# Queries, keys and values by seven block products instead of eight

## The chip, the cores and the metric

The kernel runs on one core of a Trainium2 chip. The metric is the device time of one execution in microseconds. Three runs of the kernel before took 2755.23, 2757.62 and 2761.46 us, with the median at 2757.62.

## What is computed

A backbone of two layers over 1024 latent tokens of width 1024 on a grid of 16 x 64, with 256 context tokens as a prefix. Layer 0 mixes by a gated linear recurrence and a Fourier block, layer 1 by attention in a neighbourhood plus all context keys. Each layer ends with a SwiGLU FFN of hidden size 2816. Everything is float32. The change concerns the start of layer 1's mixer:

```python
def _na_mixer(hx, hc, w_qkv, rpb, w_out, need_ctx):
    qkv = (hx @ w_qkv).reshape(B, R, GRID_W, 3, NA_HEADS, NA_HD)
    q = qkv[:, :, :, 0] * scale
    k = qkv[:, :, :, 1]
    v = qkv[:, :, :, 2]
    qkv_c = (hc @ w_qkv).reshape(B, L, 3, NA_HEADS, NA_HD)
    ...   # scores of 8 x 16 neighbours and 256 context keys, softmax, values, output projection
```

hx is the modulated RMSNorm of the tokens (1024 x 1024), hc that of the context, and w_qkv is 1024 x 3072. Of the context only keys and values are used.

## The kernel before

All products are float32 made of two parts each: an operand is split into a rounded part hi and the rest lo, and mm3 (lines 342 to 346) issues three products, hi with hi, hi with lo and lo with hi, into one bank of PSUM. split (line 308) makes hi on ScalarE (line 310) and lo on VectorE (line 311). A split operand of 512 columns is a tile of 4 KB a partition. 28 of these, called u, make the pool units; wide token rows and loaded blocks take the same tiles. Weights arrive in four staging tiles r of 2 KB, loaded by SP's queue and split into u ahead of their use; class Ahead keeps the loads four and the splits two items ahead. In PSUM the pool ps_main has four banks each for the tags d and g.

The kernel is written as a program of tiles. A planner orders the instructions of each engine by readiness and by program order and sets the waits; memory of a closed pool is used again as soon as the tiles that lay there are done. Pools stack from a left and a right side of SBUF.

The stages in order are: layer 0's mixer, its output projection, gate and up (ffn_up), down (ffn_down), queries, keys and values (qkv), attention, its output projection, and layer 1's FFN. ffn_up and layer 1's down stage (ffn_down1) already use seven block products for eight: Blocks makes the token operands B11, B21, B22 and the combinations T1 to T4 (first for tokens 0 to 511, second for 512 to 1023), Weights makes the sums S1 to S4 from the gate and up columns on GpSimd and splits them, and the loop of ffn_up forms seven products of four contraction tiles each and adds them up on VectorE and GpSimd.

ffn_down(0) multiplies in tok_block: a first block of tokens 0 to 511 with the context, then tokens 512 to 1023. Between its products it runs fillers, one every few steps: in the first block the modulation vectors of layer 1 (mods), in the second turn_steps, which load the finished rows of tokens 0 to 511 and of the context, normalise them (norm_scale), turn them by TensorE (line 1074) and split them after the modulation.

qkv then goes over two token blocks. For each block, 16 tiles of 128 columns of queries and keys are taken in turn, with 8 contraction tiles each (lines 1343 to 1359), the context's 256 columns behind the keys; then the values by tok_block, for which the tokens are the stationary operand. In the first block's values, turn_steps for tokens 512 to 1023 runs as filler. Every weight is loaded and split twice, once for each block. Outputs are split and stored in DRAM as qd, kd and vd. oT, attention's output of 32 KB, is allocated at qkv's start on the left.

attention (line 1375) opens its own pools on the left (qd, kd, bias, s, ot, vd, pt, in this order of memory) and loads for each head queries and keys (prep, line 1406), on SP's queue, by the planner as early as their buffers are free. Its TensorE order is fixed by hand (pin): scores of two tiles, transposes of the weights after softmax, products with the values.

Of the kernel before, what the change touches and what calls it, by code (L numbers as in the profile page):

```python
# [16 lines left out]
P = 128  # L17
D = 1024
T = 1024
# [77 lines left out]
class Blocks:  # L97
# [3 lines left out]
    def __init__(self, kern, l):  # L101
        self.kern, self.l, self.u = kern, l, {}
# [12 lines left out]
    def vectors(self, k):  # L115
        return self.kern.G[self.l][1][:, 0, k:k + 1], self.kern.mt[self.l][:, 3, 0, k:k + 1]
# [6 lines left out]
    def first(self, rows):  # L123

        kern = self.kern
        nc = kern.nc
        xs = [rows[m] for m in range(4)]
        self.kept = []
        for k in range(4):
            r = kern.row()  # L130
            c11, b21 = r[:, :512], r[:, 512:]
            self.kept.append((c11, b21))
            ps = self.turned(xs, k)
            scale, bias = self.vectors(k)
            u = self.unit("B11", k)
            nc.scalar.activation(c11, ps, AF.Copy, scale=scale)
            self.modulated(ps, k, u[:, 0])
            nc.vector.scalar_tensor_tensor(u[:, 1], c11, bias, u[:, 0].bitcast(F32), op0=ALU.add, op1=ALU.subtract)
            self.modulated(self.turned(xs, k + 4), k + 4, b21)
            u = self.unit("B21", k)  # L140
            kern.split(b21, u[:, 0], u[:, 1], "dve")

    def second(self, rows):
# [5 lines left out]
        for k in range(4):  # L149
            r = kern.row()  # L150
# [18 lines left out]
class Weights:  # L169
# [38 lines left out]
    def up(self):  # L208
# [3 lines left out]
        self.u.update({f"S{i}": (u, 0) for i, u in self.s.items()})  # L212

# [50 lines left out]
class Kernel:  # L264
# [797 lines left out]
    def turn_steps(self, ms, src, l, i, units):  # L1062

        nc = self.nc
        n = len(ms) * P
        st = {}

        def load():
            st["x"] = self.load_scale(ms, src)

        def turn(k):
            ps = self.t(self.pp, [P, 512], F32, "g")
            for q, m in enumerate(ms):
                nc.tensor.transpose(ps[:, q * P:(q + 1) * P], st["x"][m][:, k * P:(k + 1) * P], self.ident)
            b = k * n % 512
            if b == 0:
                st["u"] = self.unit()
            u = st["u"][:, :, b:b + n]
            self.modulate_split(ps, l, i, k, ((0, n, int(ms[0] < 0)),), None, u[:, 0], u[:, 1])
            units.setdefault(k, []).append(u)  # L1080

        return [load] + [lambda k=k: turn(k) for k in range(KD)]
# [108 lines left out]
    def ffn_down(self, l, blocks, hd, src, store, gg, fillers=((), ()), start=(0, 0), every=(1, 1)):  # L1191
# [13 lines left out]
        for b, ms in enumerate(blocks):  # L1205
            def act(k, half, b=b, ms=ms):
# [125 lines left out]
    def qkv(self, first, src):  # L1332
        nc, a = self.nc, self.a
        pp = self.pp
        self.kst = ExitStack()
        op_ = self.pool("oT", side="left", stack=self.kst)
        self.oT = [self.t(op_, [P, T], F32, f"oT{j}") for j in range(8)]
        self.vd = self.t(self.dram, [P, 10, 2, 4, 256], F32, "vd")
        self.qd = [self.t(self.dram, [P, 2, T], F32, f"qd{j}") for j in range(8)]
        self.kd = [self.t(self.dram, [P, 2, TT], F32, f"kd{j}") for j in range(8)]  # L1340
        units = first
        for bi, ms in enumerate((BLOCKS[0] + CTX, BLOCKS[1])):
            for mt in range(16):
                w = [self.ws.take() for _ in range(2)]
                for part in range(2 if bi == 0 and mt >= 8 else 1):
# [223 lines left out]
    def run(self):  # L1569
# [64 lines left out]
        def store2(m, x):  # L1634
            nc.sync.dma_start(out=self.x2[m], in_=x)
# [191 lines left out]
```

## Time and profile before

| | us |
|---|---|
| median of three runs | 2757.62 |
| the profiled execution | 2757.91 |
| its span | 2756.1 |
| TensorE busy in it | 2630.0 |
| VectorE busy | 1625.6 |
| ScalarE busy | 1222.3 |
| GpSimd busy | 881.9 |

PE is TensorE's products, PEld its loads of the stationary operand, which run beside them; DVE is VectorE, ACT ScalarE, POOL GpSimd, SP the engine that issues the DMAs. Times in the rows are microseconds from the span's start, unless ns is written. A product's busy time includes its way through the array, so that two in a row overlap; the distance of their starts is what one costs. Behind a row in brackets stands the idle time of the engine before it, and what ended it.

### The profile page before, as it was taken

The page shows a single profiled execution, that of the slowest core. Times are in us where ns is not written, and L with a number is a line of the kernel's source. Part 1 is how long each engine was busy: PE and PEld are TensorE (multiplying, and loading weights), DVE is VectorE, ACT ScalarE, POOL GpSimd, SP SyncE. Part 2 cuts the span into 40 slices and gives each one's busy share as a digit, 9 for nine tenths or more (in the row PEclk, how much of TensorE's full clock was granted, in tenths as well). Part 3 has the DMA queues.
Part 4 walks back from the last instruction along what each step waited for, and adds up shares of the span by engine and source line. Part 5 has one row for each costly group of instructions (what it writes and reads, how often), then busy time and mean ns, then how long its engine had stood idle before and what let it go on. Part 6 is the DMA issues. An engine that isn't in the chain of part 4 may idle for free. (4 is left out here: it accounts for less than half of the span.)

```text
span 2756.1 us, 36241 instructions
## 1 busy us (share of the span) xinstructions
PE 2630.0 (95%) x12914; PEld 2146.4 (78%) x12914; DVE 1625.6 (59%) x2506; ACT 1222.3 (44%) x2201; POOL 881.9 (32%) x794
## 2 busy tenths in 40 slices
PE   7999999899999999899999999999997999999997
PEld 3677577688888887777878887998875888888786
DVE  3765285866543445675552433877767666556966
ACT  3676264422232223343532333988754333333443
POOL 1000014544444341002010000777536554542911
PEclk9999999899999999999999999999999999999999
DMA  7333472233221227855344485777441333235524
GB/s 245 107 113 124 134 250 86 73 104 112 78 75 67 73 67 233 268 163 211 108 172 169 162 254 187 189 179 172 141 138 54 108 107 115 88 108 185 200 100 145
DMA packets 185574, 390.41 MB, mean 142 GB/s; under 512 B 19761, under 2 KB 50097, under 8 KB 183346
## 3 DMA queue, kind: packets, MB, share of 16 engines
q1 hardware_dynamic: 185394, 388.10, 43.5%
q8 instruction: 102, 1.67, 0.2%
q14 instruction: 78, 0.64, 0.1%
HBM read 302.57 MB, written 85.46 MB: 141 GB/s over the span
## 5 line engine op out<-in xcount | busy, mean ns | idle before, releaser
L345 PE MATMUL d<-u,u 128*128 128x512 f32 (+1 forms) x864 | 335.0, 388 | 5.4 <-DVE u L311 5.4
L344 PE MATMUL d<-u,u 128*128 128x512 f32 (+1 forms) x864 | 335.0, 390 | 4.5 <-DVE y L248 2.6
L346 PE MATMUL d<-u,u 128*128 128x512 f32 (+1 forms) x864 | 333.2, 386 | 0.0
L311 DVE TENSOR_TENSOR u<-r,u 128x512 fp32r<-128x512 f32 x309 | 231.5, 765 | 78.2 <-ACT u L310 76.6
L310 ACT ACTIVATE u<-r 128x512 fp32r<-128x512 f32 x309 | 187.7, 626 | 176.0 <-PE d L346 42.9
L346 PE MATMUL g<-u,u 128*128 128x512 f32 x604 | 236.2, 391 | 4.3 <-DVE u L311 4.3
L345 PE MATMUL g<-u,u 128*128 128x512 f32 x604 | 236.5, 391 | 1.8 <-DVE u L311 1.8
L344 PE MATMUL g<-u,u 128*128 128x512 f32 x604 | 236.6, 392 | 0.0
L244 POOL TENSOR_TENSOR ss<-ss 128x1 f32<-128x1 f32 x36 | 13.3, 371 | 654.7 <-ACT junk L242 654.5
L311 DVE TENSOR_TENSOR s<-r,s 128x512 fp32r<-128x512 f32 x176 | 139.0, 794 | 127.3 <-ACT s L310 126.7
L345 PE MATMUL g<-u,s 128*128 128x512 f32 x528 | 208.2, 394 | 4.9 <-POOL u L166 4.8
L344 PE MATMUL g<-u,s 128*128 128x512 f32 x528 | 207.5, 394 | 2.1 <-ACT u L121 1.9
L346 PE MATMUL g<-u,s 128*128 128x512 f32 x528 | 207.0, 392 | 0.0
L344 PEld LDWEIGHTS d<-u,u 128*128 128x128 f32 x864 | 164.4, 190 | 48.1 <-ACT u L310 9.5
L310 ACT ACTIVATE s<-r 128x512 fp32r<-128x512 f32 x176 | 108.6, 629 | 209.1 <-PE g L346 144.5
L345 PEld LDWEIGHTS d<-u,u 128*128 128x128 f32 x864 | 164.5, 190 | 39.9 <-DVE u L311 9.4
L346 PEld LDWEIGHTS d<-u,u 128*128 128x128 f32 x864 | 164.5, 190 | 31.7
L1476 POOL TENSOR_TENSOR s<-s,sm 128x640 f32<-128x640 f32 (+1 forms) x128 | 151.0, 1200 | 61.9 <-DVE sm L1472 56.2
L192 POOL TENSOR_TENSOR r<-rg,ru 128x512 f32<-128x512 f32 x44 | 59.5, 1352 | 305.3 <-DMA rg<-in_w_gu_dram 123.1
L344 PE MATMUL d<-u,ga 128*128 128x512 f32 x352 | 139.3, 396 | 0.1
L346 PE MATMUL d<-u,ga 128*128 128x512 f32 x352 | 138.2, 393 | 0.6 <-DVE ga L311 0.6
L1152 POOL TENSOR_TENSOR ub<-ub,ua 128x512 f32<-128x512 f32 x44 | 72.9, 1657 | 204.6 <-DVE ua L1151 199.0
(407 smaller groups left out, 6511.3 us busy)
## 6 DMA issues: line engine op xcount, KB each, us to landing
mraw<-in_w_mod_dram SPq DMA_DIRECT2D x192, 256.0 KB, 3.6
rg<-in_w_gu_dram SPq DMA_DIRECT2D x44, 512.0 KB, 3.6
ru<-in_w_gu_dram SPq DMA_DIRECT2D x44, 512.0 KB, 3.7
r<-in_w_down_dram SPq DMA_DIRECT2D x88, 256.0 KB, 3.4
x<-x SPq DMA_DIRECT2D x40, 512.0 KB, 4.3
r<-in_w_qk_dram SPq DMA_DIRECT2D x64, 256.0 KB, 3.8
qd<-qd SPq DMA_DIRECT2D x32, 512.0 KB, 11.1
r<-in_w_out_dram SPq DMA_DIRECT2D x48, 256.0 KB, 3.2
```

Source lines behind the costliest of these rows:

```text
L192: pool(rs[3], rg[:, h1], ru[:, h1], op=ALU.subtract)
L244: nc.gpsimd.tensor_tensor(st, ss[:, 0:1], ss[:, 1:2], op=ALU.add)
L310: i = nc.scalar.activation(hi, src, AF.Copy) if eng == "act" else nc.vector.tensor_copy(hi, src)
L311: j = nc.vector.tensor_tensor(lo, src, hi.bitcast(F32), op=ALU.subtract)
L344: nc.tensor.matmul(ps, lhs[0], rhs[0], start=start, stop=False)
L345: nc.tensor.matmul(ps, lhs[0], rhs[1], start=False, stop=False)
L346: nc.tensor.matmul(ps, lhs[1], rhs[0], start=False, stop=stop)
L1152: pool(ub, ub, ua, op=add)
L1476: pin(nc.gpsimd.tensor_tensor(s, s, sm.to_broadcast([P, nl + L]), op=ALU.mult))
```

## The change

The tokens are cut into two halves of 512, the contraction into two halves of 512, and the columns into two: for a pair of 128 query and 128 key columns by query and key (class Pairs, eight pairs j), for the values by column halves of 512. The eight products of blocks become seven of sums of blocks, with the same combinations as in ffn_up. Values come first now (values_of), then queries and keys (queries_and_keys). Each weight is loaded once, or twice where it enters a sum of the values.

Blocks.first is cut into four steps (first_of), which run as fillers in the second block of ffn_down for tokens 0 to 511; turn_steps keeps the context. The rows of tokens 512 to 1023 are normalised where ffn_down stores them (store2) and stay in SBUF; Blocks.second turns and combines them between the two contraction halves of the values. The first product of the values, B11 and B21 with the first 512 columns, runs in d banks together with the context's values in g; the context's second half follows alone; then T1, T2, B22, T3 and T4, each with four weights. The sums of the values' weights are made on GpSimd from the staging tiles (value_loads).

The pools are set in another order: y before mraw, so that mraw can be closed between the two blocks of ffn_down (between) for a pool vu of the values' split weights on the right; a pool v for the values on the left in place of y; after it, on the same memory, the pool uq for the weights of queries and keys (rg, ru, ga, s4, s1, s3, s2, up, 40 KB) and qt above it (p1, ha, hb, ua, ub, and two output tiles qo). oT is allocated in attention. The diff, cut to its core:

```diff
+class Pairs(Weights):
+    def load(self, j):
+        self.raw = [kern.t(kern.uw, [P, 1024], F32, n) for n in ("rg", "ru")]
+        for i in range(2):
+            kern.nc.sync.dma_start(out=self.raw[i], in_=kern.a["w_qk"][8 * i + j])
...
+    def value_loads(self, unit, s1):
+        def sum1(k):
+            a, b = raw(0, 1, k), raw(1, 1, k)
+            pool(s1(k), a, b, op=add)
+            return later(s1(k))
...
+        plain = [lambda r=r, c=c, k=k: self.wload(src(r, c, k), unit) for c in range(2) for r in range(2) for k in range(4)]
+        sums = [lambda f=f, k=k: f(k) for f in (sum1, sum2, sum4, sum3) for k in range(4)]
+        return plain + sums + [lambda k=k: self.wload(src(1, 1, k), unit) for k in range(4)]
...
+    def values_of(self, vp, tb, rows, cx):
+        p1, p5 = ([self.t(vp, [P, 512], F32, f"{n}{i}") for i in range(4)] for n in ("p", "q"))
...
+        g = banks("g", 2)
+        for r in range(2):
+            d = banks("d")
+            for k in range(4):
+                w = self.ws.take()
+                mm(d, tb.u[("B11", "B21")[r], k], w, k == 0, k == 3)
+                mm(g, cx[4 * r + k], w, r == 0 and k == 0, r == 1 and k == 3)
+            if r == 0:
+                for i in range(4):
+                    nc.scalar.activation(p1[i], d[i], AF.Copy)
+                tb.second(rows)
...
+        for i, ps in product("g", "T1"):
+            nc.scalar.activation(p5[i], ps, AF.Copy)
...
+        for i, ps in product("g", "T4"):
+            dve(p1[i], ps, p1[i], op=add)
+            put(i, 1, p1[i])
...
+    def queries_and_keys(self, W, T, cx):
+        for j in range(8):
+            if more:
+                W.load(j + 1)
+            ps = prod("A11", "B11", "d")
+            nc.scalar.activation(p1, ps, AF.Copy)
+            ps = prod("A12", "B21", "d")
+            dve(ha, ps, p1, op=add)
+            put(ha, 0.125, q[:, :, 0:512])
+            if more:
+                W.sums()
+                W.gate()
+            ps = prod("S4", "B22", "g")
+            nc.scalar.activation(ub, ps, AF.Copy)
+            p5 = prod("S1", "T1", "d")
+            dve(ub, p5, ub, op=add)
+            p7 = prod("S3", "T3", "g")
+            ps = prod("S2", "T2", "g")
+            if more:
+                W.splits()
+            dve(ua, ps, p1, op=add)
+            pool(ub, ub, ua, op=add)
+            put(ub, 0.125, q[:, :, 512:])
+            dve(ua, p7, ua, op=add)
+            dve(hb, p5, ua, op=add)
+            put(hb, 1.0, kt[:, :, L + 512:])
+            ps = prod("A22", "T4", "g")
+            dve(ua, ps, ua, op=add)
+            put(ua, 1.0, kt[:, :, L:L + 512])
...
+                self.mm3(ps[:, :L], (u[:, 0, c], u[:, 1, c]), (cx[k][:, 0], cx[k][:, 1]), k == 0, k == KD - 1)
+            put(ps[:, :L], 1.0, kt[:, :, 0:L])
+            if more:
+                W.up()
...
         def store2(m, x):
             nc.sync.dma_start(out=self.x2[m], in_=x)
+            if m >= 4:
+                rows[m] = self.row()
+                self.norm_scale(x, rows[m])
```

## Rows read from the trace of the kernel before

**Rows 1.** The page: the span, and busy time by engine with instructions.
```profile
span 2756.1 us, 36241 instructions
PE 2630.0 (95%) x12914; PEld 2146.4 (78%) x12914; DVE 1625.6 (59%) x2506; ACT 1222.3 (44%) x2201; POOL 881.9 (32%) x794
```

**Rows 2.** Busy by stretch: length, PE, PEld, DVE, ACT, POOL, PEclk, DMA share, GB/s.
```profile
1393.00:1552.00 159.00, 154.67 (x772) 130.87 (x771) 60.74 (x94) 46.64 (x90) 14.89 (x22) 0.98 0.48 167
1552.00:1712.00 160.00, 159.27 (x709) 131.64 (x708) 56.64 (x90) 49.44 (x88) 0.64 (x4) 1.00 0.65 211
...
2125.00:2500.00 375.00, 374.99 (x1654) 309.99 (x1653) 229.43 (x282) 125.35 (x197) 194.56 (x141) 1.00 0.30 105
```

**Rows 3.** In order of time, TensorE at the stage's end: start, us, instruction.
```profile
1704.71 0.39 PE L344 MATMUL g<-u,u 128*128 128x512 f32 x1
...
1710.61 0.39 PE L346 MATMUL g<-u,u 128*128 128x512 f32 x1
1711.73 0.50 PE L1437 MATMUL s<-kd,qd 128*128 128x256 f32 x2 [0.73 <-DVE u L1367]
```

**Rows 4.** In order of time, TensorE and VectorE at the stage's start.
```profile
1393.35 0.48 PE L344 MATMUL g<-u,u 128*128 128x512 f32 x1
...
1403.85 0.79 PE L346 MATMUL g<-u,u 128*128 128x512 f32 x1 [4.33 <-DVE u L311]
...
1401.16 1.40 DVE L248 SCALAR_TENSOR_TENSOR y<-d,rstd,gg 128x512 f32<-128x512 f32 x2
```

**Rows 5.** Groups by form, TensorE, 1393 to 1712: count, busy, mean ns, idle.
```profile
L344 PE MATMUL g<-u,u 128*128 128x512 f32 x320 | 125.8, 393 | 0.0
...
L346 PE MATMUL d<-u,u 128*128 128x512 f32 x97 | 37.8, 390 | 0.0
...
L346 PE MATMUL d<-u,u 128*128 128x256 f32 x64 | 18.1, 283 | 0.0
```

**Rows 6.** Groups by form, VectorE: 1393 to 1712 first, then 2125 to 2500.
```profile
L311 DVE TENSOR_TENSOR u<-r,u 128x512 fp32r<-128x512 f32 x94 | 62.4, 703 | 10.6 <-ACT u L310 9.8
...
L311 DVE TENSOR_TENSOR s<-r,s 128x512 fp32r<-128x512 f32 x83 | 71.9, 870 | 61.1 <-ACT s L310 60.6
L311 DVE TENSOR_TENSOR ga<-rg,ga 128x1024 fp32r<-128x1024 f32 x19 | 23.2, 1219 | 1.5 <-ACT ga L310 1.4
...
L1151 DVE TENSOR_TENSOR ua<-g,p 128x512 f32<-128x512 f32 x21 | 14.5, 690 | 16.2 <-PE g L346 16.2
```

**Rows 7.** Blocks.second on VectorE: order of time, group (465 to 520), line 166.
```profile
494.49 0.69 DVE L154 TENSOR_TENSOR u<-u,u 128x512 fp32r<-128x512 f32 x1 [1.90 <-ACT u L121]
...
497.57 2.30 DVE L311 TENSOR_TENSOR ga<-rg,ga 128x1024 fp32r<-128x1024 f32 x1
...
515.48 0.68 DVE L154 TENSOR_TENSOR u<-u,u 128x512 fp32r<-128x512 f32 x1
...
L166 DVE TENSOR_TENSOR u<-y,u 128x512 fp32r<-128x512 f32 x10 | 11.3, 1142 | 0.5 <-ACT u L165 0.2
...
L166 DVE TENSOR_TENSOR u<-y,u x24: 677/1352/1781, 497.0 to 2122.6; 128x512 fp32r<-128x512 f32 x24
```

**Rows 8.** Waits of TensorE, 2050 to 2125: us in total, times, longest.
```profile
PE g L345 <- POOL u L166: 4.3, 1, 4.3
```

**Rows 9.** In order of time, TensorE at the start of layer 1's gate and up.
```profile
2092.50 0.50 PE L344 MATMUL d<-u,s 128*128 128x512 f32 x1
2092.83 0.39 PE L344 MATMUL d<-u,ga 128*128 128x512 f32 x1
```

**Rows 10.** Attention's loads of queries: issue (ns, first and last start), and landing.
```profile
L1414 SPq DMA_DIRECT2D qd<-qd x32: 488/596/1939, 1594.9 to 1933.5; - x32
...
DMA to landing us min/median/max: 6.3/11.1/14.0
```

**Rows 11.** Busy by stretch, columns as in rows 2, around a hole of TensorE.
```profile
1140.00:1145.00 5.00, 0.26 (x1) 0.26 (x2) 2.27 (x5) 0.00 (x0) 0.00 (x0) 0.50 0.91 326
1145.00:1150.00 5.00, 5.00 (x15) 4.05 (x15) 3.02 (x9) 0.00 (x0) 0.00 (x0) 0.51 0.81 252
```

More of the change, by code (lines that the diff above doesn't have):

```diff
@@ L1189, in ffn_up, with ffn_down @@
         st.close()
-    def ffn_down(self, l, blocks, hd, src, store, gg, fillers=((), ()), start=(0, 0), every=(1, 1)):
+    def ffn_down(self, l, blocks, hd, src, store, gg, fillers=((), ()), start=(0, 0), every=(1, 1), between=None):
         def load(b, i):
@@ L1205, in ffn_down @@
         for b, ms in enumerate(blocks):
+            if b and between:
+                between()
             def act(k, half, b=b, ms=ms):
@@ L1381, in pin @@
             return i
+        self.kst = ExitStack()
+        op_ = self.pool("oT", side="left", stack=self.kst)
+        self.oT = [self.t(op_, [P, T], F32, f"oT{j}") for j in range(8)]
         sps = self.pool("ps_s", bufs=1, space=PSUM, stack=st)
@@ L1629, in run @@
         cst.close()
+        self.open_y(6, ny=6)
         self.open_mraw()
-        self.open_y(6, ny=6)
         gg = [self.gain_rows(0, 2, w, self.yp, self.pp, "g") for w in range(2)]
+        cst = ExitStack()
+        cp = self.pool("cxq", side="right", stack=cst)
+        vst = ExitStack()
+        vp = {}
+        rows.clear()
+        cx = []
+        self.vd = self.t(self.dram, [P, 10, 2, 4, 256], F32, "vd")
+        self.qd = [self.t(self.dram, [P, 2, T], F32, f"qd{j}") for j in range(8)]
@@ new lines, in between, with vrow, s1_of @@
+        def between():
+            self.mraw_stack.close()
+            vp["u"] = self.pool("vu", bufs=4, side="right", stack=vst)
+        def vrow():
+            return self.t(vp["v"], [P, 1024], F32, "s1", bufs=2)
+        s1 = {}
+        def s1_of(k):
+            if k // 2 not in s1:
+                s1[k // 2] = vrow()
+            return s1[k // 2][:, 512 * (k % 2):512 * (k % 2) + 512]
+        tb = Blocks(self, 1, 0, vrow)
+        down = self.wrows(self.a["w_down"][0], 0, NF)
+        self.ws = Ahead(down * 2 + self.value_loads(lambda: self.t(vp["u"], [P, 2, 512], F32R, "u"), s1_of), DW, DS[1])
@@ L1642, in run @@
         self.du = DUS[1]
-        self.ffn_down(0, (BLOCKS[0] + CTX, BLOCKS[1]), hd, x1, store2, gg, (mods[9:], turns), (0, TS), (2, 1))
+        self.ffn_down(0, (BLOCKS[0] + CTX, BLOCKS[1]), hd, x1, store2, gg,
+                      (mods[9:], self.turn_steps(tb, rows, x2, cx, cp)), (0, TS), (2, 1), between)
         self.y_stack.close()
-        self.mraw_stack.close()
-        self.qkv(nx, x2)
+        self.u_stack = ExitStack()
+        vp["v"] = self.yp = self.pool("v", side="left", stack=self.u_stack)
@@ L1647, in run @@
+        vrow()
+        self.values_of(vp["v"], tb, rows, cx)
+        self.u_stack.close()
+        vst.close()
+        self.u_stack = ExitStack()
+        self.uw = self.pool("uq", side="left", stack=self.u_stack)
+        W = Pairs(self, 1, True)
+        W.load(0)
+        W.sums()
+        W.gate()
+        W.splits()
+        W.up()
+        self.queries_and_keys(W, tb, cx)
+        self.u_stack.close()
+        cst.close()
         self.u2.close()
```

204 lines of the change are left out of this document (127 added, 77 removed).

## The prediction

> **What bounds the kernel now.** I read the page's totals first: TensorE is busy for 95% of a span of 2756.1 us [rows 1]. The profiled execution took 2757.9 us, 1.8 us more than its span and 0.3 us more than the median of the three runs (2757.62), so I make the sum against 2757.9. An average says nothing of one stage, so the next view is the busy time by stretch. The queries, keys and values run from 1393 to 1712; TensorE is busy for 154.67 of the first 159 us and 159.27 of the last 160, at a granted clock of 0.98 and 1.00, while VectorE is busy for 61 and 57, ScalarE for 47 and 49 and GpSimd for 15 and 1 [rows 2]. A busy TensorE need not be a full one, so I look at starts in the list in order of time: from 1704.71 to 1710.61 there are 26 steps in 5.90 us, 0.227 us for a product of 512 columns, without a hole [rows 3]. One hole stands at the start of the stage, 4.33 us, for a split of weights that VectorE has queued behind the end of the FFN [rows 4]. So the stage costs what its products cost: 3 x 320 on g, by the code 3 x 96 on d (one group shows a record of the FFN's end as well) and 3 x 64 of 256 columns [rows 5]; 1248 x 0.227 + 192 x 0.12 is 306 of its 318 us. Fewer products are time gained, wherever TensorE finds its next operands ready.
>
> **What the change removes.** Queries and keys of the tokens were 16 x 2 x 8 x 3 = 768 products and become 8 x 7 x 4 x 3 = 672. Values of the tokens were 4 x 2 x 2 x 8 x 3 = 384 and become 7 x 4 x 4 x 3 = 336. Context products stay (96 and 192 short ones), and so do the 80 transposes. So 144 products go: 144 x 0.227 = **32.7 us**. Weight splits hardly change (96 of 512 columns before; 36 for values and 8 x 8 for queries and keys after).
>
> **What it adds, seam by seam.** Added are the sums of weights on GpSimd (16 for values, 32 for queries and keys), Blocks.second (20 VectorE instructions on two SBUF operands, 4 on PSUM, 28 ScalarE, 12 GpSimd), and sums of products on VectorE (20 and 48).
>
> *Queries and keys, inner loop.* The loop copies the gate and up loop. Layer 1's is the nearest row: 375 us with TensorE busy for 374.99 and VectorE for 229 [rows 2]. Here one j is 84 x 0.227 + 24 x 0.12 = 22 us of TensorE. VectorE has two splits of 1024 columns, four of 512, six sums and five puts: 2 x 1.22 + 4 x 0.87 + 11 x 0.69, some 13.5 us [rows 6], or 61% as in layer 1. I take 0.5 us of waits in all, bounds 0 to 4.
>
> *(a) Start of the values.* The first four d banks still hold the FFN's last half; VectorE releases the last two between 1401.16 and 1402.56, some 9 us after the FFN's last product, which the stage's first follows at 1393.35 [rows 4]. Before, the stage began in g banks and waited 4.33 us for a weight. Now context products in g give 2 x 1.4 us of cover at once. The four norms that were in the value fillers move up into this seam: 4 squares on ScalarE and 4 multiplications on VectorE ahead of the next splits, two small GpSimd steps each, and the weight splits queue behind them; in exchange a load of each row and its wait on SP's queue are gone. I take 2 us more than before, bounds 0 (the cover suffices) and 5.
>
> *(b) Blocks.second inside the values.* In layer 0 three of its four steps took VectorE from 494.49 to 515.48, 21.0 us, in which one foreign split of 2.30 stands [rows 7]: 6.2 us a step, 25 for four. Between the first half of the contraction and T1, TensorE has 72 products (16.3 us), 32 transposes (some 3.5) and the second context pass (48, 10.9): 31 us. VectorE has in that time 25 + 13 weight splits + 8 puts and 4 sums: 25 + 13 x 0.87 + 8 x 0.75 + 2.8 = 45 us [rows 6, 7]. Some 14 us are over, but half of the splits of T2, T3 and T4 can be done during T1. T1 itself also waits for sums of weights, each of which takes two of the four staging tiles. I take 8 us, bounds 3 and 14. Where second stands in the gate and up stage, its own waits on TensorE include one of 4.3 us, under 5 us of cover [rows 8].
>
> The Trainium skill, "SBUF — State Buffer", section Who interferes with whom, states that a VectorE instruction with two SBUF inputs and a GpSimd instruction that reads SBUF exclude each other for their whole length. The trace agrees in kind: the split of weights takes 703 ns on average where GpSimd is nearly idle, 870 in layer 1's loop, and second's own subtraction has a median of 1352 [rows 6, 7]. By that rule VectorE's time in (b) would be its time alone plus nearly all of GpSimd's, and the wait would be 14 us or more rather than 8; this is the mechanism of the third rival below.
>
> *(c) Values to queries.* By the order and sizes of the allocations, the tile ga of the first j lies exactly over p0 to p3, the running sums of the values. It can be written only when the last put of the values has read them: four sums and four splits on VectorE (4 x 1.4, the first 2 us before the last product ends), then a gate split, 1.22 us of VectorE behind ScalarE's half of it [rows 6]. That would be 6 to 7 us of idle TensorE. But S4, S1, S3 and S2 lie over tiles that are free earlier, and in layer 1 the program's order already puts a product of s (2092.50) ahead of products of ga (2092.83) [rows 9]. I take 2, bounds 0 and 7.
>
> *(d) Queries to attention.* Before, the values came last and attention's pools lay on free memory: its first loads were issued from 1594.9 on, over 100 us ahead [rows 10], and scores began 1.12 us after the last product [rows 3]. Now the weights' pool lies under oT and the first query buffer: 32 KB of oT, then qd; the pool's last tile, up, takes bytes 32 K to 40 K, exactly the first qd buffer, and the key buffer lies over ub and a put. up is read by the last products of the stage (context keys). So on SP's queue both query loads of head 0, and the loads behind them, stand until TensorE has finished. Such a load takes 6.3 us at least and 11.1 in the middle from issue to landing [rows 10]; less the old 1.1, the bounds are 5 and 13. I take 9. Nobody else has work then. Where TensorE was busy for 0.26 of 5 us (1140 to 1145), the granted clock was 0.50 there and 0.51 in the next 5, that is 1.2 GHz instead of 2.4 [rows 11]; here it costs little, since scores are followed by VectorE.
>
> Elsewhere: the fillers of the FFN's second half are 14 instead of 18, with 3 ScalarE and 3 VectorE instructions for a pair of blocks instead of 2 and 4, and swapping the pools of mraw and y moves only who reuses what. I cost both at nothing, since TensorE's 2.7 us a step cover them; if that fails, it is 1 to 2 us.
>
> **Sum.** -32.7 + 2 + 8 + 2 + 0.5 + 9 = -11.2: **2747 us**. All low bounds give 8 us of waits (2733), all high ones 43 (2768).
>
> **Rivals.**
> *The seams are hidden* (chance 0.20). For it: the order of instructions is laid out by readiness, so T1 and the S products can fill in, and in the layer 1 loop nothing waits. If head 0's loads find their buffers free earlier, (d) is 0 and only (a) and (b) remain at 2 and 3: -27.7, **2730**. Against it: up lies where the first query buffer lies.
>
> *No difference* (0.15). Two of the seams, (b) and (d), come at their upper bounds: 14 + 13 + 4.5 = 31.5 against 32.7, **2757**. For it: Blocks.second has taken VectorE wholly before. Against it: both bounds at once.
>
> *The values become bound by VectorE, slower* (0.15). Of VectorE's instructions in the values 72 have two SBUF operands (36 weight splits, 16 puts, 20 of second); 28 read PSUM (19.3 us), and 9 us of the FFN's end lie ahead. TensorE has 102 us there. With the other seams at 13.5 us, the gain is gone once the values take 19.2 us longer than that, 121.2 us: from a mean of (121.2 - 28.3) / 72 = **1.29 us** on. The rows give 0.70, 0.87, 1.14 and, as second's median, 1.35 [rows 6, 7]. At 1.35 and (d) at 13: 97 + 28 - 102 = 23.6, with 17.5 of the other seams 41, **2766**. Against it: GpSimd is not busy throughout.
>
> That the products do not fall by 144 is excluded by the code's own counts.
>
> **How the numbers follow.** The forecast, waits of 14 to 27 us at the seams (2739 to 2752), has 0.50. About 0.2%, 5.5 us, is what can be told from no change. Faster by more: the forecast and hidden seams, 0.70; within it, 0.15; slower, 0.15. The range leaves out the outer part of the first and the last rival: 2731 to 2765.
>
> **What would show it.** In the profile after: 1104 products of 512 columns in the stage at 0.227 us; TensorE waits on VectorE or GpSimd of some 8 us before T1; a hole of 6 to 13 us ahead of the first scores, ended by the landing of qd; in the queries and keys hardly any wait. I am wrong if the hole ahead of the scores is absent, if the two-operand VectorE instructions in the values average over 1.29 us, or if waits appear in the FFN before the stage.

## The result, and the profile after

The changed kernel takes 2797.59 us (median of four runs, 2794.26 to 2800.63) against 2756.43 for the kernel before in the same session: a ratio of 1.0149, 95% interval 1.0125 to 1.0174. It is 41 us slower where 11 us faster was forecast, and lies outside the range (2731 to 2765).

The page's totals of the changed kernel, as in [rows 1]:

```profile
span 2793.3 us, 36142 instructions
PE 2608.2 (93%) x12770; PEld 2122.2 (76%) x12770; DVE 1704.0 (61%) x2566; ACT 1255.6 (45%) x2237; POOL 999.1 (36%) x870
```

The products did fall by 144 (12914 to 12770), and TensorE's busy time by 21.8 us. The span rose by 37.2 us all the same, so TensorE idles 59 us more. The busy time by stretch (columns as in [rows 2]) says where:

```profile
1393.00:1430.00 37.00, 29.51 (x126) 22.43 (x125) 18.84 (x23) 18.33 (x34) 18.33 (x25) 0.95 0.26 93
1430.00:1475.00 45.00, 34.11 (x129) 25.83 (x130) 34.31 (x42) 21.67 (x36) 18.20 (x12) 0.89 0.47 164
1475.00:1530.00 55.00, 49.90 (x209) 39.68 (x207) 36.23 (x41) 17.27 (x29) 29.18 (x20) 0.97 0.49 167
1530.00:1550.00 20.00, 7.95 (x25) 5.67 (x26) 9.25 (x9) 6.78 (x10) 7.27 (x4) 0.66 0.42 158
1550.00:1715.00 165.00, 165.00 (x806) 139.64 (x806) 92.22 (x125) 58.83 (x94) 56.32 (x35) 1.00 0.45 155
1715.00:1750.00 35.00, 5.43 (x37) 4.83 (x35) 4.97 (x8) 3.56 (x5) 4.03 (x15) 0.61 0.82 220
```

The loop of queries and keys is full (165.00 of 165). The losses are the values (1393 to 1530), the seam behind them, and the seam ahead of the scores. TensorE's waits in the first two and in the third (us in total, times, longest) name what ended them:

```profile
PE d L357 <- ACT ga L323: 12.4, 1, 12.4
PE g L358 <- DVE u L324: 6.6, 2, 4.0
PE d L357 <- DVE y L261: 5.7, 4, 2.3
PE g L113 <- DVE y L162: 3.2, 2, 2.3
...
PE s L1588 <- DMA qd<-qd: 29.6, 1, 29.6
```

In the table each length is a difference of starts in TensorE's list in order of time: the values from their first product to their last, the hole behind them, queries and keys, the hole ahead of the first scores. In h_all the last products of the values stand behind the first two of the queries, so the values run to those. The whole for the kernel before, 1393.35 to 1711.73, is 318.4 us [rows 3, 4].

| kernel | values | hole | queries, keys | hole | whole |
|---|---|---|---|---|---|
| changed kernel | 136.4 | 12.8 | 178.7 | 29.9 | 357.7 |
| e_order | 135.6 | 14.5 | 178.7 | 14.0 | 342.8 |
| e_rg | 140.0 | 8.8 | 177.7 | 30.1 | 356.5 |
| e_defer | 131.6 | 14.4 | 178.7 | 29.4 | 354.0 |
| e_banks | 136.2 | 14.5 | 178.7 | 29.7 | 359.0 |
| e_pool | 131.0 | 14.4 | 178.7 | 29.4 | 353.5 |
| e_nopool | 126.3 | 13.1 | 178.7 | 29.3 | 347.4 |
| e_left | 121.4 | 14.3 | 178.7 | 28.9 | 343.4 |
| f_d | 137.4 | 12.6 | 178.7 | 10.5 | 339.2 |
| f_all | 140.9 | 0.2 | 182.9 | 10.2 | 334.3 |
| g_all | 128.8 | 0.2 | 180.6 | 0.1 | 309.8 |
| h_all | 120.2 | - | 189.3 | 0.1 | 309.7 |
| i_all | 125.0 | 0.2 | 175.4 | 0.1 | 300.7 |

With the products alone the whole should have been 318.4 - 32.7 = 285.7; the changed kernel has 72 us on top. Fifteen executions of the kernel before in one session lie between 2742.88 and 2762.61 us, and the kernels from e_order to f_d were run once each, so these are judged by this table and not by their times. In it, too, a part that an edit leaves alone moves by 1 to 2 us (the hole behind the values is 12.8, 14.5 and 12.6 in the changed kernel, e_order and f_d). The profiled execution of f_all was the fastest of its four, that of h_all the slowest of its ten.

### The profile page after: what moved, and what is told of

Read it like the earlier page. It is cut to its first block, busy times and chain, and to the rows that moved or that the text cites. A ratio compares the mean times of both kernels' runs of the same rounds, so it can differ in the third digit from the quotient of the medians.

```text
span 2793.3 us, 36142 instructions
## 1 busy us (share of the span) xinstructions
PE 2608.2 (93%) x12770; PEld 2122.2 (76%) x12770; DVE 1704.0 (61%) x2566; ACT 1255.6 (45%) x2237; POOL 999.1 (36%) x870
## 5 line engine op out<-in xcount | busy, mean ns | idle before, releaser
L357 PE MATMUL d<-u,u 128*128 128x512 f32 x768 | 304.7, 399 | 10.4 <-DVE y L261 8.4
L358 PE MATMUL d<-u,u 128*128 128x512 f32 x768 | 305.5, 398 | 7.0 <-DVE u L324 7.0
L359 PE MATMUL d<-u,u 128*128 128x512 f32 x768 | 303.1, 395 | 0.1
L324 DVE TENSOR_TENSOR s<-r,s 128x512 fp32r<-128x512 f32 x208 | 159.8, 776 | 159.9 <-ACT s L323 154.5
L257 POOL TENSOR_TENSOR ss<-ss 128x1 f32<-128x1 f32 x36 | 12.6, 350 | 670.6 <-ACT junk L255 670.4
L358 PE MATMUL g<-u,s 128*128 128x512 f32 x624 | 245.2, 393 | 5.1 <-POOL u L169 4.3
L357 PE MATMUL g<-u,s 128*128 128x512 f32 x624 | 244.8, 393 | 2.6 <-ACT u L122 1.9
L359 PE MATMUL g<-u,s 128*128 128x512 f32 x624 | 244.3, 392 | 0.0
L323 ACT ACTIVATE s<-r 128x512 fp32r<-128x512 f32 x208 | 127.6, 629 | 252.1 <-PE g L359 154.7
L324 DVE TENSOR_TENSOR u<-r,u 128x512 fp32r<-128x512 f32 x241 | 192.4, 806 | 75.0 <-ACT u L323 74.3
L323 ACT ACTIVATE u<-r 128x512 fp32r<-128x512 f32 x241 | 149.2, 627 | 188.7 <-PE d L359 48.1
L195 POOL TENSOR_TENSOR r<-rg,ru 128x512 f32<-128x512 f32 x52 | 75.6, 1454 | 389.0 <-DMA rg<-in_w_gu_dram 124.8
L357 PEld LDWEIGHTS d<-u,u 128*128 128x128 f32 x768 | 146.2, 191 | 54.1 <-DVE y L261 10.9
L358 PEld LDWEIGHTS d<-u,u 128*128 128x128 f32 x768 | 146.7, 191 | 40.8 <-DVE u L324 11.8
L357 PE MATMUL d<-u,ga 128*128 128x512 f32 x416 | 164.6, 396 | 12.5 <-ACT ga L323 12.4
L359 PEld LDWEIGHTS d<-u,u 128*128 128x128 f32 x768 | 146.7, 191 | 31.5 <-DVE u L324 1.0
L359 PE MATMUL d<-u,ga 128*128 128x512 f32 x416 | 163.1, 392 | 0.7 <-DVE ga L324 0.6
L358 PE MATMUL d<-u,ga 128*128 128x512 f32 x416 | 163.3, 392 | 0.0
L358 PEld LDWEIGHTS g<-u,s 128*128 128x128 f32 x624 | 118.1, 189 | 30.7 <-POOL u L169 5.3
L357 PEld LDWEIGHTS g<-u,s 128*128 128x128 f32 x624 | 118.0, 189 | 29.2 <-ACT u L122 3.5
```

The source lines that it names most:

```text
L195: pool(rs[3], rg[:, h1], ru[:, h1], op=ALU.subtract)
L257: nc.gpsimd.tensor_tensor(st, ss[:, 0:1], ss[:, 1:2], op=ALU.add)
L323: i = nc.scalar.activation(hi, src, AF.Copy) if eng == "act" else nc.vector.tensor_copy(hi, src)
L324: j = nc.vector.tensor_tensor(lo, src, hi.bitcast(F32), op=ALU.subtract)
L357: nc.tensor.matmul(ps, lhs[0], rhs[0], start=start, stop=False)
L358: nc.tensor.matmul(ps, lhs[0], rhs[1], start=False, stop=False)
```

## Experiments: the hole ahead of the scores

SP's queue in the changed kernel, in order of time (start, us from there to the last issue's end, issue):

```profile
1706.17 12.75 SPq L1471 DMA_DIRECT2D qd<-qo  x2
1719.01 0.57 SPq L1572 DMA_DIRECT2D vd<-vd  x1
1720.45 3.40 SPq L1471 DMA_DIRECT2D kd<-qo  x2
...
1730.17 0.53 SPq L1471 DMA_DIRECT2D kd<-qo  x1
...
1732.16 0.57 SPq L1572 DMA_DIRECT2D vd<-vd  x1
1732.85 1.02 SPq L1564 DMA_DIRECT2D kd<-kd  x1
1733.90 0.78 SPq L1565 DMA_DIRECT2D qd<-qd  x1
...
1736.28 1.92 SPq L1565 DMA_DIRECT2D qd<-qd  x1
```

TensorE's last product, and ScalarE's half of the last store's split:

```profile
1720.14 0.28 PE L359 MATMUL d<-cx,up 128*128 128x256 f32 x1
1729.30 0.38 ACT L1469 ACTIVATE qo<-d 128x256 fp32r<-128x256 f32 x1 [6.72 <-DMA kd<-qo]
```

The last product starts at 1720.14. The stage's last store is issued 10.0 us later: it waits for a row buffer, of which there are two, and so for an earlier store to land. That store, issued at 1720.45 right behind a load of values of 1280 KB, took 8.7 us to land, where those of its size before this load took 3.0 to 3.4. Behind the last store on the same queue stand biases and a second load of values of 1280 KB, and only then the loads that the scores need.

**e_order** gives attention's pools other places:

```diff
-ORDER = 'qd kd bias s ot vd pt'
+ORDER = 'ot pt pad128 s pad256 bias pad1280 qd kd vd'
```

> Edit: the attention pools stand in another order, so that the first query and key rows of attention lie over token units that are free early in the last block, and not over the two up units and the row buffers that the last block's stores read. Nothing of the arithmetic changes. Theory (the 29.6 us hole before the first scores is order: the loads of head 0 stand behind the last stores of the block and behind a second 1.28 MB load of values): half of head 0's loads now stand ahead of the last store, the rest still behind it, so the hole falls to 10 to 15 us and the time by 15 to 20 us, to about 2780. Rival (the transfers themselves fill the DMA engines, which were 0.94 busy in the hole): the same bytes must land before the scores whatever their order, the hole stays at 25 us or more and the time within 5 us of the changed kernel.

**f_d** does this too, and changes the last stores:

```diff
-            u = self.t(tp, [P, 2, 512], F32R, "qo", bufs=2)
+            u = self.t(tp, [P, 2, 512], F32R, "qo", bufs=3)
...
-            put(hb, 1.0, kt[:, :, L + 512:])
+            put(hb, 1.0, kt[:, :, L + 512:], nc.sync if more else nc.gpsimd)
```

> Edit: e_order's places for the attention pools, and besides: the last three stores of keys of the last block go out on GpSimd's queue, and the row buffer has three places instead of two. Theory (what was left of the hole in e_order, 14.0 us, is the second half of head 0's loads standing behind the last store on SyncE's queue): the hole falls to 4 to 8 us and the time by 22 to 27 us against the changed kernel, to about 2773. Rival (the bytes themselves: some 2.7 MB must land in the hole): it stays at 12 us or more.

Measured: 2783.26 and 2779.92 us. TensorE's wait for the landing, in e_order

```profile
PE s L1592 <- DMA qd<-qd: 13.7, 1, 13.7
```

and in f_d

```profile
PE s L1593 <- DMA qd<-qd: 10.2, 1, 10.2
```

The same bytes move, and the hole falls from 29.9 to 14.0 us with other places alone, as the theory had it (10 to 15); the whole falls by 14.9, just short of its 15 to 20. Order was the larger part, and the rival (transfers alone, 25 us or more) falls. f_d, at 10.5, stayed above its 4 to 8, though, and below its rival's 12: one store, that of ub, still stood on SP's queue ahead of the loads (issued from 1722.37). g_all, below, sends it elsewhere too, and the hole is 0.1.

## Experiments: the hole behind the values

SP's queue and ScalarE in the changed kernel, in order of time:

```profile
1515.58 20.25 SPq L1400 DMA_DIRECT2D vd<-vo  x10
1535.88 0.42 SPq L225 DMA_DIRECT2D rg<-in_w_qk_dram  x1
...
1534.13 0.63 ACT L1398 ACTIVATE vo<-p 128x512 fp32r<-128x512 f32 x1 [0.96 <-DMA vd<-vo]
1540.35 1.06 ACT L323 ACTIVATE ga<-rg 128x1024 fp32r<-128x1024 f32 x1 [5.59 <-DMA rg<-in_w_qk_dram]
```

The values' last product starts at 1528.66. A put is the split of one result and its store. The last put waits until 1534.13 for a place of the store buffer, and the gate's raw rows are loaded behind the stores.

**e_rg** loads them sooner, into a pool of their own:

```diff
-        self.raw = [kern.t(kern.uw, [P, 1024], F32, n) for n in ("rg", "ru")]
+        self.raw = [kern.t(kern.rw, [P, 1024], F32, n) for n in ("rg", "ru")]
...
             put(4 + i, 0, u4[i])
+        early()
```

> Edit: the two raw rows of the first query and key weight block get a pool of their own that lives on below the values' pool, and are loaded after the fifth product of the values instead of behind the last value stores. Theory (the 12.8 us hole between values and queries is the raw row's load, issued 6.8 us into the hole because the queue stood behind stores that wait for their buffers): the gate still lies over p0 to p3, which the last puts read, so its split starts some 2 us after the last put; the hole falls to 5 to 9 us, the time by 4 to 8 us. Rival (the gate's place alone sets the hole): the hole stays at 11 to 13 us.

Measured: 2789.78 us. The hole fell to 8.8 us, as the theory had it (5 to 9), but the values grew by 3.6, so the two together stayed (149.2 and 148.8). It doesn't settle the price, and it shows that the load was only a third of the hole: in e_rg the gate's split comes at 1538.29, right behind the last put, and that put (1536.90) again waits for a store's landing. In f_all the gate has a place of its own besides, is split while product T4 runs (1513.21), and the hole is 0.2 us.

## Experiments: the values

**e_banks** swaps the banks at the start:

```diff
-        g = banks("g", 2)
+        g = banks("d", 2)
...
-            d = banks("d")
+            d = banks("g")
```

> Edit: at the start of the values stage the token products take the banks called g and the context products those called d, and the transposes of the second half of the token sums go to d; in after it is the other way round. Nothing of the arithmetic changes. Theory (the four gaps of 0.8 to 2.7 us between 1393 and 1414 are products waiting for a d bank that VectorE has yet to empty of sums of the stage before): 4 to 5 us fewer waits there, and as much less time. Rival (the products wait for VectorE in whatever bank): the gaps reappear within the same stretch under the other name, and the time stays within 2 us.

Measured: 2800.12 us, values 136.2. The rival holds: the four waits of 1393 to 1414, 5.7 us in all, became two of 3.3 and 1.1, for the same release of banks, and one of 3.7 for the last row of the stage before. A bank swap moves TensorE forward to the next thing that isn't ready.

**e_defer** does eight splits later:

```diff
+                if self.i == 0 and n in self.later[k]:
+                    continue
...
+        tb.finish("T2")
         for i, ps in product("g", "T1"):
             nc.scalar.activation(p5[i], ps, AF.Copy)
+        tb.finish("T4")
```

> Edit: of the second half of the token sums in the values stage, the T2 and T4 combinations are not split into high and low parts at once but kept in 32-bit tiles, T2's until just ahead of product T1 and T4's until after it. The same work is done, 8 splits later. Theory (VectorE, 14.93 of 15 us busy in 1430 to 1445, is what the products of the values stage wait for): the waits of that stage fall by 5 to 10 us and so does the time. Rival (the waits are those for banks and for the weights' units, and VectorE only happens to be busy): the waits only move from the second half of the sums to the products after it, and the time stays within 2 us.

Measured: 2788.43 us, values 131.6: 4.8 us less, just short of the expected 5 to 10. The hole behind is 1.6 longer, but it is so in e_order too, which leaves the values alone. The whole fell by 3.7, beyond the rival's 2; with parts that move by 1 to 2 us by themselves this leans to the theory and does not settle it.

**e_left** says what the sums inside the values cost in all:

```diff
+            if self.i == 0:
+                u = self.unit("T1", k)
+                kern.split(r1, u[:, 0], u[:, 1])
+                for n in ("T2", "T3", "T4"):
+                    self.u[n, k] = u
+                continue
```

> Edit to the changed kernel: the combinations T2, T3 and T4 of the second half of the token sums are left out, with their splits, and the products take T1's units in their place; this run computes other numbers than the reference, and serves to time the stage without those 36 instructions of three engines. Theory (of the 36 us by which the values stage is longer than its products, the token sums inside it are the largest part): values go from 136 to 112 to 120 us. Rival (the waits at the start, for the weights and for the stores make up the excess, and the sums only stand beside them): values stay above 128 us.

Measured: 2779.26 us, values 121.4, so 15.0 us, just short of the theory's band and far from the rival's. Some 20 us over the products (432 x 0.227) and transposes (3.5) remain. TensorE's waits in them are 5.8 us for banks at the start, 5.9 for splits and 0.2 for a put; most of the rest are products that start further apart.

That holds for the changed kernel too: of the 34.8 us by which its values exceed products and transposes, TensorE's waits are 22.5. Behind several of them the granted clock is lower for a while: 0.66 from 1402 to 1407 and from 1432 to 1437, 0.69 from 1457 to 1462, 0.67 from 1467 to 1472. Where TensorE is busy throughout, 5 us at 0.67 hold 16 products and 5 us at 1.00 hold 24:

```profile
1467.00:1472.00 5.00, 5.00 (x16) 3.51 (x15) 1.99 (x3) 2.23 (x4) 1.29 (x1) 0.67 0.97 330
...
1492.00:1497.00 5.00, 5.00 (x24) 4.14 (x23) 2.40 (x3) 0.63 (x1) 5.00 (x4) 1.00 0.34 106
```

**e_pool** and **e_nopool** move GpSimd's work to VectorE, the first the twelve instructions of the token sums, the second the weight sums and sums of products as well:

```diff
+        if self.i == 0:
+            pool = dve
...
-        pool = self.nc.gpsimd.tensor_tensor
+        pool = self.nc.vector.tensor_tensor
```

> Edit: in the second half of the token sums of the values stage, the twelve instructions of GpSimd (two sums and one low part of T3 for each of four blocks) are done on VectorE instead. Theory (the low parts on VectorE take 1.50 us each there, since GpSimd reads two operands at the same time; alone they take 0.68): VectorE gets 12 instructions more, yet its low parts fall to 0.7 to 1.0 us, a block of the sums goes from 7.7 to about 7 us, and the waits of the values stage fall by 2 to 5 us. Rival (the two engines don't slow each other, the 1.50 us are another thing): 12 instructions more at 0.7 to 1.5 us make the stage 8 to 18 us longer.

> Edit to the changed kernel, nothing else: every sum that GpSimd makes in the values stage (twelve of the token combinations, sixteen weight sums, eight sums of products) is made on VectorE in its place. Theory (beside GpSimd a VectorE subtraction takes 1.5 to 1.75 us, alone 0.68): VectorE gets 36 instructions more, 24 us at 0.68, and gets back 25 to 35 us, since none of its instructions is slowed, and nobody waits for GpSimd's 1.3 to 1.7 us each; the values stage goes from 136 to 120 to 129 us. Rival (the slow instructions of VectorE have another cause, or VectorE's 24 us more stand on the path): values take 140 us or more.

Measured: 2793.13 and 2784.87 us, values 131.0 and 126.3. VectorE's groups from 1393 to 1475, of the changed kernel (between the bars: busy us, mean ns)

```profile
L169 DVE TENSOR_TENSOR u<-y,u 128x512 fp32r<-128x512 f32 x12 | 17.6, 1502 | 0.0
L324 DVE TENSOR_TENSOR u<-r,u 128x512 fp32r<-128x512 f32 x12 | 9.9, 864 | 0.0
```

and of e_nopool

```profile
L171 DVE TENSOR_TENSOR u<-y,u 128x512 fp32r<-128x512 f32 x16 | 10.3, 684 | 0.3 <-ACT u L170 0.3
L326 DVE TENSOR_TENSOR u<-r,u 128x512 fp32r<-128x512 f32 x12 | 7.6, 683 | 0.6 <-ACT u L325 0.6
```

Sixteen instructions take 10.3 us where twelve took 17.6. The first subtraction of a block in e_pool:

```profile
1429.05 0.68 DVE L159 TENSOR_TENSOR u<-s,u 128x512 fp32r<-128x512 f32 x1
...
1434.57 0.68 DVE L159 TENSOR_TENSOR u<-s,u 128x512 fp32r<-128x512 f32 x1
...
1440.05 0.68 DVE L159 TENSOR_TENSOR u<-s,u 128x512 fp32r<-128x512 f32 x1
```

A block of the sums takes 5.5 us there, in which VectorE does nine instructions. In the changed kernel it takes 7.7 (1430.14, 1437.86, 1445.61) for six of them and one foreign split of 1.77, so 5.9 without that. VectorE is full in both, and three instructions more take less time. The values became 5.4 us shorter in e_pool, a little more than the expected 2 to 5, and 10.1 in e_nopool, within the 120 to 129; both rivals, by which they would be longer, fall. What GpSimd did beside VectorE cost more than it saved. For the combinations alone e_pool gives the share: 5.4 of the 15.0 us of e_left come back although all of the work is still done. How much of the other 4.7 of e_nopool is VectorE's slowing, and how much waiting for GpSimd's results, is not separated.

## Experiments: all seams together

**f_all** joins f_d, the gate's place, and a second half of the sums in the order in which the products ask for it, all on VectorE:

```diff
-                tb.second(rows)
+                tb.second_a(rows)      # r1 and T1 of all four blocks
+        tb.second_b(rows)              # B22, T2
...
+        t1 = product("g", "T1")
+        tb.second_c()                  # T3, T4
...
+        W.gate()
+        ps = product("g", "T4")
+        W.sums()
```

> Edit: f_d, and in the values stage: (1) the second half of the token sums is done in the order in which the products ask for it: T1 for all four blocks first, then B22 and T2, then, beside product T1, T3 and T4, all of it on VectorE and with T3 made from T2 in place of the second transposed row; (2) the first gate and raw rows of the queries and keys have a pool of their own, are loaded after product B22 and split ahead of product T4. The products are the same. Theory (all of the loss is at seams, and VectorE's order within the sums): values 136 down to 110 to 122 us, the hole behind them 12.8 to 1 to 3, the hole ahead of the scores to 4 to 8, so the stage from values to first scores goes from 357.7 to 300 to 313 us, below before's 318.4, and the time to 2740 to 2755, faster than before by 0 to 0.6%. Rival (VectorE is the bound of the values stage, whatever the order: the same splits now delay the products behind T1): values stay above 130 us and the time above 2762.

Measured: 2772.2 us, ratio 1.0082 (1.0057 to 1.0106). The hole behind the values went, the one ahead of the scores stayed at f_d's 10, and the values did not get shorter: 140.9 us, where the rival had above 130 and a time above 2762. Its waits, 1380 to 1545:

```profile
PE g L413 <- DVE u L379: 8.4, 4, 7.1
...
PE g L412 <- DVE vo L1454: 6.1, 2, 5.7
PE g L412 <- ACT s L378: 3.4, 1, 3.4
```

The 5.7 us ahead of T1 are a bank that a put has yet to read. A place of the store buffer came free at 1454.88; ScalarE stood until 1454.90 for a weight sum of GpSimd, and VectorE's half of the split began at 1458.46, behind two instructions of 1.75 us. The 7.1 us are weights of T4, split on VectorE behind puts that wait for GpSimd's sums. So reordering the sums alone did not pay: puts, GpSimd's sums and a busy VectorE came next, and this run does not part them.

**g_all** gives the store buffer a third place, moves the sums behind B21's products, two GpSimd sums to VectorE, and ub's store to GpSimd's queue:

```diff
-            u = self.t(vp, [P, 2, 512], F32R, "vo", bufs=2)
+            u = self.t(vp, [P, 2, 512], F32R, "vo", bufs=3)
...
-            pool(p5[i], p1[i], p5[i], op=add)
+            dve(p5[i], p1[i], p5[i], op=add)
```

> Edit: f_all, and besides: the store of ub's queries in the last block goes out on GpSimd's queue too; the values' store buffer has three places instead of two (the 32-bit results of the first half are put together in it); the second half of the token sums is issued behind both products of B11 and B21 instead of between them, with its transposes and the context's products in the banks d and the token products in g; the two sums of the results behind T2 and T3 go from GpSimd to VectorE. The products are the same. Theory (in f_all the values stage kept its 141 us since the pieces in turn waited for a free place of the store buffer, 5.7 us ahead of T1 and up to 6.9 on ScalarE behind T3, for the last rows of the stage before, and behind sums of GpSimd; and the scores' loads stood behind ub's store): values 141 down to 112 to 125 us, queries and keys back to 178 to 180, the hole ahead of the scores 10.2 down to 0 to 4, so from values to scores 295 to 308 us and the time 2733 to 2750, faster than before. Rival (the stores of values and the loads of the weights fill the DMA engines in this stage, and no buffer or order helps): values stay above 132 us, and the time above 2752.

Measured: 2755.18 us, ratio 1.0014 (1.0003 to 1.0026). Values and whole (128.8 and 309.8) came out just above the expectation; the time missed it by more, because a wait had gone elsewhere. TensorE's waits from 1690 on, then GpSimd and VectorE in order of time:

```profile
PE s L1659 <- DVE mx L1684: 15.2, 4, 12.9
...
1715.10 0.69 POOL L1537 DMA_DIRECT2D kd<-qo  x1 [9.43 <-DVE qo L1536]
...
1716.17 0.45 POOL L1617 MEMSET be<- 128x256 f32 x1
...
1716.40 0.69 DVE L1684 CUSTOM_DVE_ANT_0 s<-s,be 128x512 f32<-128x512 f32 x1 [1.59 <-POOL be L1616]
```

The first scores start at once, but their maximum needs the zeros of the edge bias, and GpSimd writes these behind a store that it can issue only 9.4 us later, when a row buffer has come free. The queue that took SP's stores is an engine with work of its own.

**h_all** writes these zeros first, gives the last two stores their own places, and puts each block's piece of the sums between products:

```diff
+        for k in range(4):
+            tb.step_a(rows, k)
+            for z in (2 * k, 2 * k + 1):
+                mm(g, cx[z], self.ws.take(), z == 0, z == KD - 1)
```

> Edit: g_all, and besides: each block's piece of the second half of the token sums is issued between the products that can cover it (T1's pieces between the context's second products, B22's and T2's between the blocks of T1, T3's and T4's behind T2's first blocks); the copies of the first partial sums go from ScalarE to VectorE; the splits of the first two weight sums of the queries and keys (S4, S1) are made ahead of the last value stores, in a place of their own; in the last block the last two stores have places of their own, and the zeros of the edge bias are written first on GpSimd. The products are the same. Theory (in g_all the second scores waited 13.3 us since GpSimd, held at its last store by the row buffer, wrote the edge zeros only at 1716; S4 cost 3.4; and VectorE was 18.7 of 20 us busy in 1430 to 1450, while the products stood): the 13.3 us fall to 1 to 4, the 3.4 to 0 to 1, values from 128.8 to 108 to 120 us, the time from 2755 to 2722 to 2738, faster than before by 0.6 to 1.2%. Rival (the values stage stays at VectorE's and the stores' pace, 125 us or more): only the two other waits go, and the time stays at 2740 or above.

Measured: 2750.17 us, ratio 0.9995 (0.998 to 1.001). It missed, and the rival's 125 us or more came true: the 120.2 us of the table end at the first of the queries, but the 48 products of T4 now stand behind it, the last of them 134.4 us after the start, and the whole stayed at 309.7. The wait for the maximum went, and one of 6.3 us, of the first transpose for GpSimd, took its place. VectorE and GpSimd at the wait of T2:

```profile
1473.07 0.68 DVE L165 TENSOR_TENSOR u<-ga,u 128x512 fp32r<-128x512 f32 x1
1473.67 1.78 DVE L375 TENSOR_TENSOR u<-s,u 128x512 fp32r<-128x512 f32 x1
1475.37 1.78 DVE L171 SCALAR_TENSOR_TENSOR u<-s,mt,u 128x512 f32<-128x512 f32 x1
1477.07 1.75 DVE L162 TENSOR_TENSOR s<-ga,s 128x512 f32<-128x512 f32 x1
...
1473.60 3.00 POOL L1420 TENSOR_TENSOR rg<-rg,r 128x512 f32<-128x512 f32 x2 [4.51 <-DMA r<-in_w_qkv_dram]
1476.57 3.38 POOL L1420 TENSOR_TENSOR ru<-ru,r 128x512 f32<-128x512 f32 x2
...
1483.27 3.39 POOL L1425 TENSOR_TENSOR r<-r,ru 128x512 f32<-128x512 f32 x2
```

From the instruction at which GpSimd's row of weight sums begins, each instruction of VectorE on two operands in SBUF takes 1.75 to 1.78 us instead of 0.68 to 0.74, until the row ends at 1486.7.

**i_all** moves these sixteen sums to VectorE, too, lets two blocks of tokens run ahead of the first context products, and takes the turned probabilities off the row buffers:

```diff
-        pool = self.nc.gpsimd.tensor_tensor
+        pool = self.nc.vector.tensor_tensor
         add, sub = ALU.add, ALU.subtract
         w = self.a["w_qkv"]
```

> Edit: h_all, and besides: the sixteen weight sums of the values stage (S1 to S4, four blocks each) go from GpSimd to VectorE; the first two blocks' token products of B11 stand ahead of the first two context products; the copies of the first partial sums are back on ScalarE; the tiles of turned probabilities of attention lie over token units and not over the last block's row buffers. The products are the same. Theory (in h_all nine subtractions of VectorE in 1473 to 1487 took 1.75 us instead of 0.68, while GpSimd made weight sums back to back, and T2 waited 2.9 and 4.6 us for them; the context's bank cost 3.7 us at the start; GpSimd stood at its zeros of the turned tiles until the last stores had landed, 6.3 us for the first softmax): VectorE gets 16 instructions more, yet its mean falls to 0.7 to 0.8 us and the waits at T2 to under 2 us; values go from 119 to 105 to 114 us, the first transpose after the scores comes 4 to 6 us sooner, and the time is 2728 to 2742, 0.4 to 0.9% faster than before. Rival (VectorE is full either way): values stay at 117 us or more and the time within 0.2% of before.

Measured: 2738.28 us (2729.44 to 2748.39) against 2753.59, ratio 0.9946 (0.9929 to 0.9963): faster than both kernels, with the same 12770 products as the changed one. Its totals and stretches:

```profile
span 2737.3 us, 36117 instructions
...
PE 2597.7 (95%) x12770; PEld 2118.2 (77%) x12770; DVE 1694.4 (62%) x2602; ACT 1252.2 (46%) x2233; POOL 941.9 (34%) x838
...
1430.00:1475.00 45.00, 43.72 (x206) 35.05 (x205) 38.00 (x63) 26.67 (x45) 0.00 (x0) 1.00 0.60 205
1475.00:1519.00 44.00, 37.08 (x152) 29.33 (x151) 38.67 (x60) 17.52 (x29) 6.78 (x4) 0.92 0.53 181
1519.00:1694.00 175.00, 175.00 (x864) 148.78 (x863) 97.81 (x140) 65.11 (x105) 50.32 (x40) 1.00 0.54 178
```

From 1430 to 1475 TensorE is busy for 43.72 of 45 us (34.11 in the changed kernel), with GpSimd at nothing. The whole is 300.7 us, 17.7 under before. The values, 125.0 us, didn't reach their 105 to 114, and lie above the rival's 117, though its time (within 0.2% of before) did not come: one wait of 5.7 us for a weight's split, behind sums on a full VectorE, and one of 4.0 for ScalarE's copies behind a norm, are left. i_all builds on f_d, f_all, g_all and h_all, so it shows what their edits give together, not what each is worth.

## Why the prediction was wrong, point by point

**What is removed** was right: 144 products, 0.227 us each, and the loop of queries and keys has 0.5 us of waits, as forecast (178.7 us in every kernel that didn't touch its edges). The bound was named rightly as well: TensorE, and the seams decide. The sizes of three seams were wrong.

**(d), 9 us forecast (5 to 13), 28.7 measured** (29.9 less before's 1.1). The mechanism (head 0's buffers lie over what the last products read) was right; what was mis-sized is the time from the last product to the issue. I priced the landing alone, and that was in range: the second query load was issued at 1736.28, and the scores started 13.7 us later, of 6.3 to 14.0 in [rows 10]. Before it stand 16.1 us that I had at none: 10.0 until the last store finds a row buffer, and 6.1 of biases, values and other loads on SP's queue. The step that failed was "both query loads stand until TensorE has finished": they stand until the last store has been issued.

**(c), 2 us forecast (0 to 7), 12.8 measured,** and 3 more at half clock (0.66 granted from 1530 to 1550). I priced the four last puts as VectorE's time. They waited for the store buffer's two places, and so for landings, and the raw row's load stood behind them. That products of S would go first, as in [rows 9], did not happen: their raw rows come by the same load.

**(a) and (b), 10 us forecast (3 to 19), 27 measured** (72 less the other seams). (a) was right: the four waits at the start, 5.7 us in all, are 1.4 more than before's 4.33 [rows 4], forecast 2. (b), forecast 8 and bound 14, was mis-sized: the combinations T2 to T4 alone cost 15.0 (e_left). The block's size was right: from one block's first subtraction (line 157) to the next's are 7.7 us (1430.14, 1437.86, 1445.61), with one foreign split of 1.77 in it. The step that failed is that half of the splits would slide into T1: the last stands at 1452.2, ahead of T1's first product at 1464.1. TensorE stood before that: the transposes of the next block and the context's products waited for VectorE (2.3, 0.9, 2.3 and 4.0 us), and at T1 itself only 0.7 and 1.5 us were left. Without the slide my sum gives 14. The remaining 10 or 11 of the 27 are waits for split weights and for the store buffer, and products at a lower clock, which I costed at nothing; no run separates them.

**The rule of the Trainium skill** that I set beside (b) ("SBUF — State Buffer", section Who interferes with whom) would have made it 14 us or more rather than 8. The trace agrees in kind: subtractions of 1.50 us beside GpSimd's fell to 0.68 without it, and the values by 5.4 and 10.1. That the rule's figure lies near the 15.0 of e_left proves less, since my own sum without the slide gives 14 too.

**The rivals.** The third, values bound by VectorE, had the right engine and place, and its limit of length was passed (121.2 forecast, 136.4 measured), but not by its mechanism: over the stage (1393 to 1530) the 64 instructions with two SBUF operands take 65.5 us, 1.0 each, not 1.29. VectorE is full where the transposes and the context's products wait for it (14.93 of 15 us from 1430 to 1445), and a mean over the stage hides that. No rival had three seams beyond their bounds at once.

## What to carry to other kernels

Price a seam by the whole chain on its queue: from the last product over its store, the buffer that the store needs, and everything queued in order ahead of the next stage's first load. Give that load a place that is free early, and look at what the queue that takes over the stores has to do itself. Where VectorE is the one that is waited for, GpSimd's sums beside it are no free help: count VectorE's instructions in the stretch where they are waited for, at the duration that they have beside GpSimd, and try the sums on VectorE.

## What the runs showed of the hardware

The price of running both engines is sharper than I had expected: a 128x512 subtraction of VectorE with both operands in SBUF took 0.68 us in e_nopool and 1.75 to 1.78 beside a row of GpSimd's sums of 1.5 to 1.7 us each (h_all).

In the hole ahead of the scores the granted clock was 0.50 (1.2 GHz instead of 2.4) in each 5 us from 1725 to 1750, with TensorE idle, and the 20 us around the hole behind the values had 0.66, and the first products after it started 0.43 us apart or more, instead of 0.227. A hole costs more than its length: here some 3 us more.

Stores of 512 KB issued from GpSimd's queue in f_d landed 10.1 us after issue in the middle, two from SP's queue 3.4. The former went out (1724.08, 1724.90) while head 0's loads were moving, the latter (1702.46, 1703.26) 20 us earlier, so the queue isn't shown to be the cause.
